# Preparing the S5 tables in batches of eight pairs, and a fourth dense hidden tile, in a hybrid decoder layer

## The chip, the cores and the metric

The kernel runs on one core of one Trainium2 chip. The metric is the device time of one execution in microseconds (us); where several executions were timed, their median. A profiled execution gives a span, from its first to its last recorded instruction, and a time of its own beside it.

## The reference, cut to what matters

The kernel computes one layer for 1024 prompt positions and 8 × 4 sample positions, 1056 columns in all, with 1024 features in fp32.

```python
def swiglu(h, w_gate, w_up, w_down):
    return (jax.nn.silu(h @ w_gate) * (h @ w_up)) @ w_down      # 1024 -> 2816 -> 1024
...
        x = x + 0.5 * swiglu(rmsnorm(x, ffn1_norm[i]), ffn1_w_gate[i], ffn1_w_up[i], ffn1_w_down[i])
        m, s5r, s5i, ssd1, conv1 = mixer(rmsnorm(x, mix_norm[i]), *st, *mix_params)
        x = x + m.astype(x.dtype)
        x = x + 0.5 * swiglu(rmsnorm(x, ffn2_norm[i]), ffn2_w_gate[i], ffn2_w_up[i], ffn2_w_down[i])
...
    y_prompt = rmsnorm(xp, final_norm)
```

The mixer holds a Mamba-2 part and an S5 part, a diagonal complex recurrence of 32 groups × 64 states (16 pairs of groups, two groups side by side on 128 partitions). Before the recurrence runs, tables are made from its parameters alone: powers of e^(i·angle) for 128 steps per pair (`dTab`), input and output factors (`dV`, `dW`) and a short kernel (`dT`).

## The kernel before, in words

Every fp32 product is three passes of TensorE in a rounded fp32 format: each operand is a high part (copied by ScalarE, line L158, function `act`) and a low part (subtracted by VectorE, L145, function `tt`), and the passes are high·high, high·low and low·high. So each weight tile (`wr` raw, `ws` split) and each activation tile costs one ScalarE and one VectorE instruction before TensorE can use it. All DMAs are issued by SyncE in one queue.

Each FFN has 22 hidden tiles of 128. The first `NSTD` = 3 are "old-form" tiles: gate and up weights are multiplied with all eight tiles of x in three blocks of 352 columns (`dense`, lines L307 to L309; the first tile of each FFN by `pair`, L336 to L338), 144 matmuls a tile. The other 19 go through a Strassen-Winograd scheme (`strassen`, L669 to L671): seven products of half size a tile ("unit"), each of 24 matmuls of 264 columns, so 168 a unit. Products run one after the other over all units; each needs combinations of quadrants of x ("11", "1", "21", ...), which the steps of `x_steps` make on VectorE and ScalarE and which live in the same pages (`xn`, `d`, `e`) as everything else. Behind that, `down` multiplies the hidden tiles, read back from DRAM (`dH`) by `h_fetch` and split again, with the down weights in chunks of 8, 8 and 6 hidden tiles; its evacuation (`stt`, L155) adds onto x, which `x_load` has read back.

The order is set by a clock of ticks: after every third matmul the program calls `tick()`, which issues background steps whose gap, in ticks, has run out. Two queues of steps exist; `GAP` holds the gaps by name, and `at(n, fn)` places a step n ticks on. `rs_steps` (the sums for the norm, whose last reduction is the matmul `rs_col`, L369) and `x_steps` run this way under the old-form tiles: `sums(14)` starts them 14 ticks after it is called, behind FFN1's first tile but ahead of FFN2's.

The S5 preparation (`s5_prep`) is one queue of such steps, begun 30 ticks into FFN1's `down`. After the small steps come eight slices of two pairs, each of `vees` (six VectorE operations up to `vr` and `vi`, stored to `dV`, L1191), `kern` (L1200 on TensorE, a ScalarE copy into `kt`, a VectorE addition to it, eight stores to `dT`, L1208), `doubleus` (six more, up to `wr` and `wi`) and `turn` (L1222 transposes, a copy to `we`, a store to `dW`, L1225) and two parts of `table` (L1232 copies, doublings of the table from 1 to 128 steps, one Newton step that restores unit length, a store to `dTab`, L1242). Ahead of `down`'s last chunk, `mid(2)` calls `flush()`: all steps that are still in the queue are issued there, one behind the other, before the next matmul of `down`, and the fetch of the last six hidden tiles behind them.

Of the kernel before, what the change touches and what calls it, by code (L numbers as in the profile page):

```python
# [9 lines left out]
F32 = mybir.dt.float32  # L10
# [12 lines left out]
NH = 22  # L23
# [3 lines left out]
WARM = 9  # L27
HT = T // 2
HB = HT // 2
NSTD = 3  # L30
CHUNKS = (range(0, 8), range(8, 16), range(16, NH))
EPS = 1e-6
RND = 12582912.0
# [3 lines left out]
    rs=14, rs1=1, rs2=1, a=4, b=2, h=4, a3=4, b3=2, h3=8, first=7, second=6, tail0=4, tail1=10, tail2=5, done=6, done2=6, done3=6, done4=6, add=4,  # L37
    a_dec=1, a_exp=2, a_pe=2, a_mul=2, b_pe=2, b_y=1, load_a=3, sample=6, split=18, split2=18, split_hi=5, split_lo=2, v0=1,
    v1=6, v2=6, v3=3, glu1=5, glu2=11, low=5, load=14, t0=12, t1=16, u0=8, u1=12, v_0=7, v_1=14, out=16, zout=2, s5z=6, row=4, s5a=6,
    s5b=5, s5c=6, s5d=4, prep=6, tiny=5,  # L40
)

ORDER = ((0, 1, 5, 2, 3, 6, 4, 7),) * 3 + ((0, 1, 2, 3, 4, 5, 6, 7),)
# [91 lines left out]
class Build:  # L135
# [269 lines left out]

    def std(self, wcol, rsd, first):

        nc = self.nc
        sums = lambda gap: (self.rs_steps(rsd, gap), self.x_steps(wcol))
        Gs = G, U, _ = self.Gs  # L410
        (i, w), (j, v) = self.w_next(), self.w_next()
        if not first:
            sums(14)
        self.pair(self.xn, [(w, lambda b, c0, n, p: self.act(G[:, c0:c0 + n], p, AF.Copy)),
                            (v, lambda b, c0, n, p: nc.vector.tensor_copy(U[:, c0:c0 + n], p))])
        self.w_done(i)
        self.w_done(j)
        if first:
            sums(14)

        def silu():
            self.tt(G, G, self.rs, MUL)
            self.act(G, G, AF.Silu)
            self.tt(U, U, self.rs, MUL, nc.gpsimd)

        def prod():
            self.tt(G, G, U, MUL)
            self.store(self.dH[0], G)

        for h in range(1, NSTD):  # L430
            self.std_tile(h, Gs[(h + 1) % 3], (silu, prod) if h == 1 else ())

    def std_tile(self, h, G, fix):
        nc = self.nc
        i, w = self.w_next()

        def ev_gate(b, c0, n, p):
            c = slice(c0, c0 + n)
            g = self.tmp()  # L440
# [145 lines left out]

    def strassen(self, src, ban=()):
        nc, X, st = self.nc, self.X, {}
        hs = list(range(NSTD, NH))
        n = len(hs)  # L590
        sets = [self.banks[2 * i:2 * i + 2] for i in range(3)]
        last = self.Gs[NSTD % 3]
        one, two = (t for t in self.Gs if t is not last)
        P1s, U2s, VB = one[:, 0:HT], one[:, HT:T], two[:, 0:HT]
        GB, GAs = last[:, HT:T], (two[:, HT:T], last[:, 0:HT])
# [16 lines left out]
        for i in range(1, n):  # L612
            h, p = hs[i], pos["P1", i]
# [35 lines left out]
        for p, (name, i) in enumerate(order):  # L649
            h = hs[i]  # L650
# [4 lines left out]
            a, b, c = st[i]  # L655
# [21 lines left out]
            self.wsp_free.put(w)  # L677
            if i == n - 1:
                self.released(N, src)
        assert not todo, todo.keys()  # L680

    def released(self, N, src):

        for hi, lo in self.X[N]:
            self.pages.put_half(hi, lo)
        if N == "11":
            self.wlim = self.wlims.popleft()
        if N == "21":
# [283 lines left out]
    def weights(self):  # L972
        a = self.a

        def ffn(f):
            gu, dn = a["gu" + f], a["dn" + f]
            s = [(gu[n, j], 1024) for n in range(NSTD) for j in range(2)]
            for ch in CHUNKS:
                for m in range(KD):
                    c = m % 4 * 256  # L980
                    s.append((dn[ch[0] // 2:ch[-1] // 2 + 1, m // 4, :, c:c + 256].rearrange("n p c -> p n c"), 128 * len(ch)))
            return s

        w = a["win"]
        seq = ffn("1")
# [3 lines left out]
        seq += out(1) + out(2) + out(3)  # L989
        n = len(seq)  # L990
        seq += ffn("2")
        self.wlims = deque((2 * NSTD, n + 2 * NSTD, len(seq)))
        return seq

    def s5_prep(self, F):
# [11 lines left out]
        vr, vi = f("vr", 2, 9, 16), f("vi", 2, 9, 16)  # L1008
        t1, t2 = f("t1", 288), f("t2", 288)
        wr, wi = f("wr", 2, 8, 16), f("wi", 2, 8, 16)  # L1010
        we = f("we", 2, 2, 128)
        kt = F.tile([16, 4, 240], F32, name="kt")
# [214 lines left out]
        def table(sl, part):  # L1227
            s2 = slice(2 * sl, 2 * sl + 2)
            c, s = tab[:, :, 0], tab[:, :, 1]
            if part == 0:  # L1230
                for j in range(2):
                    nc.vector.tensor_copy(tab[:, :, j, 0], e8[:, j, s2])  # L1232
            for n in ((1, 2, 4, 8, 16), (32, 64))[part]:
                sh = [128, 2, n]
                u1, u2 = (t[:, 0:2 * n].rearrange("p (g n) -> p g n", n=n) for t in (t1, t2))
                bR, bI = (t[:, :, n - 1:n].broadcast_to(sh) for t in (c, s))
                self.cmul(c[:, :, n:2 * n], s[:, :, n:2 * n], c[:, :, 0:n], s[:, :, 0:n], bR, bI, u1, u2)
                yield 2
            if part == 1:
                u1, u2 = (t[:, 0:256].rearrange("p (g n) -> p g n", g=2) for t in (t1, t2))  # L1240
                self.unit(c, s, u1, u2)
                nc.sync.dma_start(self.dTab[:, s2], tab)  # L1242
# [891 lines left out]
```

## Time and the profile before

| what | value |
|---|---|
| median of three runs | 2414.36 us (2411.01 to 2415.25) |
| profiled execution, own time | 2411.99 us |
| its span | 2410.0 us |
| mean granted clock of TensorE | 0.974 of full speed |
| TensorE busy | 2291.6 us (95%) |
| VectorE busy | 1552.2 us (64%) |
| ScalarE busy | 851.5 us (35%) |
| mean DMA traffic | 114 GB/s |

In the rows PE is TensorE, DVE VectorE, ACT ScalarE, POOL GpSimd, SPq SyncE's DMA issues. The ends of matmuls are modelled, so overlapping matmuls show longer than they are apart: their number in a stretch tells the rate, not their length. A time in brackets behind a row of the timeline is the idle time ahead of it and, behind the arrow, what ended it.

### The profile page before, as it was taken

How to read it: one execution, taken by the hardware profiler on the slowest of the kernel's cores; microseconds unless marked ns; L12 is line 12 of the kernel's file. 1: busy time of each engine (PE TensorE's matmuls, PEld its weight loads, DVE VectorE, ACT ScalarE, POOL GpSimd, SP SyncE). 2: the span in 40 equal slices, each digit the busy share in tenths (PEclk: the TensorE clock that was granted, in tenths of full speed). 3: DMA queues.
4: the chain of work that ended last, by engine and by line, in shares of the span. 5: the costliest groups of instructions: out<-in, count | busy, mean ns of one | idle time of the engine just before them, and what ended most of it. 6: DMA issues, size and time to landing. Idle time of an engine off the chain costs nothing. (4 is left out here: it accounts for less than half of the span.)

```text
span 2410.0 us, 41241 instructions
## 1 busy us (share of the span) xinstructions
PE 2291.6 (95%) x16487; PEld 2225.9 (92%) x16487; DVE 1552.2 (64%) x3298; ACT 851.5 (35%) x1382; POOL 380.4 (16%) x443
## 2 busy tenths in 40 slices
PE   9899999999954999999999999998999999999998
PEld 9799999989944989999999988998999999999997
DVE  6955555567776548688788878876955555552325
ACT  5433333322112213355545555223433333341122
POOL 1000000000000323233242455433100000000003
PEclk9899999999976999999999999999999999999999
DMA  3222122353222145454554654533122222172211
GB/s 134 80 80 80 68 84 71 124 208 98 88 59 96 52 152 164 139 181 145 173 165 146 199 157 132 172 102 124 73 76 80 76 80 73 71 277 65 89 51 72
DMA packets 192125, 274.69 MB, mean 114 GB/s; under 512 B 31551, under 2 KB 137278, under 8 KB 191934
## 3 DMA queue, kind: packets, MB, share of 16 engines
q1 hardware_dynamic: 191358, 271.54, 34.0%
q8 instruction: 129, 2.11, 0.4%
q14 instruction: 62, 0.51, 0.1%
q10 hardware_dynamic: 576, 0.52, 0.1%
HBM read 195.17 MB, written 76.84 MB: 113 GB/s over the span
## 5 line engine op out<-in xcount | busy, mean ns | idle before, releaser
L307 PE MATMUL b<-xn,ws 128*128 128x352 f32 (+3 forms) x1824 | 611.0, 335 | 4.5 <-DVE tb L145 2.5
L308 PE MATMUL b<-xn,ws 128*128 128x352 f32 (+3 forms) x1848 | 598.0, 324 | 2.8 <-DVE xn L155 2.2
L309 PE MATMUL b<-xn,ws 128*128 128x352 f32 (+3 forms) x1824 | 589.6, 323 | 0.0
L307 PEld LDWEIGHTS b<-xn,ws 128*128 128x128 f32 x1824 | 344.6, 189 | 14.9 <-DVE x L145 3.2
L308 PEld LDWEIGHTS b<-xn,ws 128*128 128x128 f32 x1848 | 350.9, 190 | 7.9 <-DVE xn L155 2.8
L670 PE MATMUL b<-xn,ws 128*128 128x264 f32 x1216 | 347.5, 286 | 1.5 <-DVE xn L145 1.5
L671 PE MATMUL b<-xn,ws 128*128 128x264 f32 x1216 | 346.7, 285 | 1.4 <-DVE ws L145 1.4
L669 PE MATMUL b<-xn,ws 128*128 128x264 f32 x1216 | 345.7, 284 | 2.1 <-ACT xn L158 1.0
L309 PEld LDWEIGHTS b<-xn,ws 128*128 128x128 f32 x1824 | 344.7, 189 | 0.0
L145 DVE TENSOR_TENSOR ws<-wr,ws 128x512 fp32r<-128x512 f32 (+3 forms) x208 | 227.0, 1093 | 107.7 <-ACT ws L158 107.7
L145 DVE TENSOR_TENSOR g<-b,g 128x264 f32<-128x264 f32 (+1 forms) x316 | 136.7, 434 | 232.0 <-PE b L671 164.5
L158 ACT ACTIVATE ws<-wr 128x512 fp32r<-128x512 f32 (+3 forms) x208 | 169.5, 818 | 273.6 <-PE b L308 238.1
L669 PEld LDWEIGHTS b<-xn,ws 128*128 128x128 f32 x1216 | 229.3, 189 | 2.7 <-ACT xn L158 1.3
L670 PEld LDWEIGHTS b<-xn,ws 128*128 128x128 f32 x1216 | 228.9, 188 | 2.3 <-DVE xn L145 2.3
L671 PEld LDWEIGHTS b<-xn,ws 128*128 128x128 f32 x1216 | 229.3, 189 | 1.9 <-DVE ws L145 1.9
L669 PE MATMUL b<-d,ws 128*128 128x264 f32 x684 | 195.8, 286 | 2.4 <-ACT ws L158 2.4
L671 PE MATMUL b<-d,ws 128*128 128x264 f32 x684 | 195.7, 286 | 0.7 <-DVE ws L145 0.7
L670 PE MATMUL b<-d,ws 128*128 128x264 f32 x684 | 196.2, 287 | 0.0
L307 PE MATMUL b<-d,ws 128*128 128x352 f32 (+2 forms) x510 | 168.2, 330 | 22.3 <-ACT d L158 16.2
L155 DVE SCALAR_TENSOR_TENSOR x<-b,x 128x352 f32<-128x352 f32 (+2 forms) x144 | 73.5, 522 | 173.0 <-PE b L309 172.7
L309 PE MATMUL b<-d,ws 128*128 128x352 f32 (+2 forms) x510 | 167.5, 328 | 1.3 <-DVE ws L145 1.3
L158 ACT ACTIVATE g<-b 128x264 f32<-128x264 f32 (+1 forms) x234 | 91.5, 391 | 216.2 <-PE b L671 211.8
(416 smaller groups left out, 4350.9 us busy)
## 6 DMA issues: line engine op xcount, KB each, us to landing
wr<-in_gu SPq DMA_DIRECT2D x67, 512.0 KB
dH<-g SPq DMA_DIRECT2D x76, 264.0 KB
wr<-in_win SPq DMA_DIRECT2D x36, 512.0 KB
wr<-in_dn SPq DMA_DIRECT2D x32, 512.0 KB
abc<-dA SPq DMA_DIRECT2D x32, 384.0 KB
xn<-dH SPq DMA_DIRECT2D x21, 528.0 KB
dC<-acc SPq DMA_DIRECT2D x20, 528.0 KB
xb<-dC SPq DMA_DIRECT2D x32, 320.0 KB
```

What stands on the lines that cost most here:

```text
L145: (eng or self.nc.vector).tensor_tensor(out, x, y, op=op)
L155: self.nc.vector.scalar_tensor_tensor(out, x, s, y, op0=op0, op1=op1)
L158: self.nc.scalar.activation(out, x, f, **k)
L307: nc.tensor.matmul(p, wh[:, kc], xh, start=(k == 0), stop=False)
L308: nc.tensor.matmul(p, wh[:, kc], xl, start=False, stop=False)
L309: nc.tensor.matmul(p, wl[:, kc], xh, start=False, stop=(k == K - 1))
L669: nc.tensor.matmul(q, wh, xh, start=(k == 0 and name in ("P1", "P2", "P5")), stop=False, skip_group_check=True)
L670: nc.tensor.matmul(q, wh, xl, start=False, stop=False, skip_group_check=True)
L671: nc.tensor.matmul(q, wl, xh, start=False, stop=(k == 3), skip_group_check=True)
```

## The change

FFN1 gets a fourth old-form tile and 18 Strassen units; FFN2 keeps three, but its sums start 40 ticks on and not 14. In the last unit of the last product, the pump of weights (`w_pump`) is called after each product that ends a unit, so that down weights are loaded and split there. The eight reloads of x now start after 24 ticks and are 18 ticks apart; before, they started at once, 6 apart. In `s5_prep` the tables are made first, eight pairs at a time in two halves, and the slices hold only `vees`, `doubleus`, `kern`, `turn`, with gaps of 4 for 6; the small steps have gaps of 3 for 5. The tiles of the slices and those of the tables share one tile, `pad`: the table (`tab`) its columns 0 to 2047, temporaries 2048 to 3071, and the slices' `vr`, `vi`, `t1`, `t2`, `wr`, `wi`, `we` columns 0 to 2175, `kt` 2176 to 3135.

```diff
-NSTD = 3
+NSTD = 4, 3
...
-    s5b=5, s5c=6, s5d=4, prep=6, tiny=5,
+    s5b=5, s5c=6, s5d=4, prep=4, tiny=3, table=2,
...
         if not first:
-            sums(14)
+            sums(40)
...
             self.wsp_free.put(w)
             if i == n - 1:
                 self.released(N, src)
+                if len(self.units[h]["done"]) == 7:
+                    self.w_pump()
...
         if N == "21":
             for m in range(KD):
-                self.at(6 * m, lambda m=m: self.x_load(m, src))
+                self.at(24 + 18 * m, lambda m=m: self.x_load(m, src))
...
+        pad = f("pad", 3136)
+        place = lambda c0, *s: pad[:, c0:c0 + int(np.prod(s))].rearrange("p (a b c) -> p a b c", b=s[1], c=s[2])
...
+        def table(half):
+            s8 = slice(8 * half, 8 * half + 8)
             c, s = tab[:, :, 0], tab[:, :, 1]
+            for j in range(2):
+                nc.vector.tensor_copy(tab[:, :, j, 0], e8[:, j, s8])
+            for n in (1, 2, 4, 8, 16, 32, 64):
+                sh = [128, 8, n]
...
+                yield GAP["table"] * (1 + n // 16)
+            for i in range(2):
+                u1, u2 = (t.rearrange("p (g n) -> p g n", g=4) for t in tmp)
+                self.unit(c[:, 4 * i:4 * i + 4], s[:, 4 * i:4 * i + 4], u1, u2)
+                yield 4 * GAP["table"]
+            nc.sync.dma_start(self.dTab[:, s8], tab)
...
+        for half in range(2):
+            L(GAP["tiny"], lambda half=half: table(half))
+        L(GAP["tiny"], lambda: nc.gpsimd.memset(kt, 0.0))
         for sl in range(8):
-            for fn in (vees, kern, doubleus, turn):
+            for fn in (vees, doubleus, kern, turn):
                 L(GAP["prep"], lambda fn=fn, sl=sl: fn(sl))
-            for part in range(2):
-                L(GAP["prep"], lambda sl=sl, part=part: table(sl, part))
```

VectorE at the end of `down`'s second chunk, before: `x7` with banks `b3` to `b5` is the chunk's last evacuation, and what follows it is a table.

```order
L145 TENSOR_TENSOR t2_4924<-tab_4931 128x32
L145 TENSOR_TENSOR tab_4931<-t1_4923,t2_4924 128x2x16
L155 SCALAR_TENSOR_TENSOR x7_96<-b3_68,x7_96 128x352
L155 SCALAR_TENSOR_TENSOR x7_96<-b4_69,x7_96 128x352
L155 SCALAR_TENSOR_TENSOR x7_96<-b5_70,x7_96 128x352
L145 TENSOR_TENSOR t1_4923<-tab_4931 128x64
L145 TENSOR_TENSOR t2_4924<-tab_4931 128x64
L145 TENSOR_TENSOR tab_4931<-t2_4924,t1_4923 128x2x32
```

VectorE at the same place after: the low parts of the last chunk's hidden tiles (`d5`, `d0`, ...) follow the evacuations directly.

```order
L155 SCALAR_TENSOR_TENSOR x7_96<-b3_68,x7_96 128x352
L155 SCALAR_TENSOR_TENSOR x7_96<-b4_69,x7_96 128x352
L155 SCALAR_TENSOR_TENSOR x7_96<-b5_70,x7_96 128x352
L145 TENSOR_TENSOR d5_163<-d5_163,d2_160 128x1056
L145 TENSOR_TENSOR d0_158<-d0_158,d8_166 128x1056
L145 TENSOR_TENSOR ws4_105<-wr1_100,ws3_104 128x768
L145 TENSOR_TENSOR d6_164<-d6_164,d3_161 128x1056
```

What moved: between the last evacuation of the second chunk and the first low part of the third, no preparation step is left.

VectorE in the new kernel where the second half of the tables ends and the first slice begins (`pad` is both; `128x512` are the Newton step of four pairs, `128x288` is `vees`).

```order
L145 TENSOR_TENSOR pad_4872<-pad_4872 128x512 x3
L152 TENSOR_SCALAR pad_4872<-pad_4872 128x512
L145 TENSOR_TENSOR pad_4872<-pad_4872 128x4x128 x2
L145 TENSOR_TENSOR d0_158<-d0_158,xn15_88 128x1056
L145 TENSOR_TENSOR d6_164<-d6_164,d3_161 128x1056
L155 SCALAR_TENSOR_TENSOR x7_96<-b3_68,x7_96 128x352
L155 SCALAR_TENSOR_TENSOR x7_96<-b4_69,x7_96 128x352
L145 TENSOR_TENSOR pad_4872<-s5par_4844,pwi_4869 128x288
L145 TENSOR_TENSOR pad_4872<-s5par_4844,pwr_4868 128x288
L145 TENSOR_TENSOR pad_4872<-pad_4872 128x288
L155 SCALAR_TENSOR_TENSOR x7_96<-b5_70,x7_96 128x352
```

And TensorE in the new kernel at the first slice's `kern` (L1206 there): it stands in the middle of `down`'s matmuls.

```order
L308 MATMUL b2_67<-xn12_85,ws2_103 128x352
L309 MATMUL b2_67<-xn11_84,ws5_106 128x352
L1206 MATMUL b6_71<-pad_4872,bbr_4866 16x128 x4
L1206 MATMUL b6_71<-pad_4872,bbi_4867 16x128 x4
L307 MATMUL b0_65<-xn13_86,ws2_103 128x352
L308 MATMUL b0_65<-xn14_87,ws2_103 128x352
```

What moved: all matmuls of `down` behind this place now stand behind the whole of both table halves on VectorE, and behind the end of the second half's store, since `vees` writes columns of `pad` that the store reads.

SyncE at the end of FFN1's Strassen part, before: reloads of x stand between the fetches of hidden tiles (`d5`, `xn4`, ...).

```order
L709 DMA xn3_76<-dH0_127 128x1056
L698 DMA x2_91<-in_x 128x1056
L709 DMA d5_163<-dH0_127 128x1056
L698 DMA x3_92<-in_x 128x1056
L246 DMA wr0_99<-in_dn1 128x4x256
L698 DMA x4_93<-in_x 128x1056
L709 DMA xn4_77<-dH0_127 128x1056
```

SyncE at the same place after:

```order
L712 DMA xn3_76<-dH0_127 128x1056
L712 DMA d5_163<-dH0_127 128x1056
L246 DMA wr0_99<-in_dn1 128x4x256
L701 DMA x0_89<-in_x 128x1056
L712 DMA xn4_77<-dH0_127 128x1056
L712 DMA xn6_79<-dH0_127 128x1056
L712 DMA xn8_81<-dH0_127 128x1056
```

What moved: one reload of x stands where five stood, the others come later in `down`, and the hidden tiles follow each other.

Counted in ticks from the start of FFN1: before, `down` begins at tick 1208, the preparation at 1238, and the last chunk at 1592, with three slices' rest still in the queue. After, `down` begins at 1200, the preparation at 1230, the two table halves stand at 1293 to 1337 and 1340 to 1384, the first slice's `vees` at 1391, its `kern` at 1401, a slice every 18 ticks from there, the last step at 1531 and the last chunk at 1584.

## Rows read from the trace of the kernel before

**Rows 1.** The page: span, TensorE's busy time.

```profile
span 2410.0 us, 41241 instructions
...
PE 2291.6 (95%) x16487; PEld 2225.9 (92%) x16487; DVE 1552.2 (64%) x3298; ACT 851.5 (35%) x1382; POOL 380.4 (16%) x443
```

**Rows 2.** Windows by stage: engines' busy us (instructions), granted clock, DMA share.

```profile
core 0: us, PE busy (x) PEld busy (x) DVE busy (x) ACT busy (x) POOL busy (x), PEclk, DMA share, GB/s
...
80.00:120.00 40.00, 28.95 (x176) 26.80 (x175) 36.61 (x59) 21.37 (x42) 1.27 (x1) 0.79 0.20 67
120.00:480.00 360.00, 360.00 (x2954) 360.00 (x2953) 188.88 (x350) 127.25 (x263) 0.00 (x0) 1.00 0.23 83
...
489.00:510.00 21.00, 15.81 (x79) 15.02 (x78) 8.82 (x9) 8.77 (x10) 0.89 (x1) 0.84 0.92 352
510.00:691.00 181.00, 179.64 (x1176) 176.31 (x1175) 135.16 (x512) 28.51 (x45) 3.55 (x16) 1.00 0.28 85
691.00:759.00 68.00, 9.40 (x67) 3.95 (x66) 51.01 (x214) 7.61 (x18) 0.00 (x0) 0.53 0.26 78
759.00:766.00 7.00, 6.60 (x29) 6.61 (x30) 6.98 (x7) 4.68 (x5) 0.00 (x0) 0.67 0.66 254
766.00:830.00 64.00, 64.00 (x399) 64.00 (x398) 36.95 (x36) 20.67 (x21) 15.74 (x6) 1.00 0.12 38
1663.00:1700.00 37.00, 32.58 (x188) 31.90 (x187) 23.52 (x33) 13.03 (x18) 7.67 (x3) 0.91 0.13 45
1742.00:1772.00 30.00, 30.00 (x247) 30.00 (x246) 21.89 (x40) 13.46 (x28) 0.00 (x0) 1.00 0.23 84
...
2134.00:2160.00 26.00, 23.12 (x134) 22.62 (x134) 15.01 (x16) 10.41 (x11) 0.00 (x0) 0.93 0.68 259
```

**Rows 3.** Timeline of TensorE around the flush: start, us, instruction, [idle before].

```profile
691.62 0.32 PE L309 MATMUL b<-d,ws 128*128 128x352 f32 x1
699.28 0.62 PE L1200 MATMUL b<-vr,bbr 64*16 64x128 f32 x8 [7.33 <-DVE vr L145]
...
717.05 0.62 PE L1200 MATMUL b<-vr,bbr 64*16 64x128 f32 x8 [11.07 <-DVE vr L145]
...
758.10 0.66 PE L307 MATMUL b<-d,ws 128*128 128x352 f32 x1 [16.19 <-ACT d L158]
```

**Rows 4.** Timeline of VectorE in the flush: one slice's rest and its table.

```profile
702.42 0.21 DVE L145 TENSOR_TENSOR kt<-kt,kd 16x64 f32<-16x64 f32 x1 [1.81 <-ACT kt L158]
...
704.93 0.23 DVE L1232 COPY tab<-e 128x2 f32<-128x2 f32 x2
705.20 0.23 DVE L145 TENSOR_TENSOR t<-tab 128x2 f32<-128x2 f32 x2
...
705.66 0.23 DVE L145 TENSOR_TENSOR t<-tab 128x2 f32<-128x2 f32 x2
...
713.15 0.76 DVE L145 TENSOR_TENSOR t<-tab 128x256 f32<-128x256 f32 x2
...
715.52 0.46 DVE L145 TENSOR_TENSOR t<-s5par,pwi 128x288 f32<-128x288 f32 x1
```

**Rows 5.** Timelines of SyncE and ScalarE behind the flush.

```profile
751.89 1.83 SPq L709 DMA_DIRECT2D d<-dH  x4
...
756.97 1.08 ACT L158 ACTIVATE d<-d 128x1056 fp32r<-128x1056 f32 x1 [13.63 <-DMA d<-dH]
```

**Rows 6.** VectorE's groups by shape, 490 to 760 us: busy us, mean ns.

```profile
L155 DVE SCALAR_TENSOR_TENSOR x<-b,x 128x352 f32<-128x352 f32 x48 | 24.6, 522 | 30.9 <-PE b L309 30.8
L145 DVE TENSOR_TENSOR ws<-wr,ws 128x1024 fp32r<-128x1024 f32 x16 | 19.4, 1220 | 11.9 <-ACT ws L158 11.9
...
L145 DVE TENSOR_TENSOR xn<-xn,xn 128x1056 fp32r<-128x1056 f32 x5 | 6.0, 1252 | 0.0
```

**Rows 7.** Timeline of TensorE at three other waits.

```profile
92.21 0.59 PE L670 MATMUL b<-e,ws 128*128 128x264 f32 x1 [3.27 <-DVE e L145]
...
493.47 0.43 PE L307 MATMUL b<-d,ws 128*128 128x352 f32 x1 [3.93 <-ACT ws L158]
...
1674.34 3.17 PE L369 MATMUL b<-ones,acc 128*128 128x1 f32 x18 [4.29 <-POOL acc L145]
```

More of the change, by code (lines that the diff above doesn't have):

```diff
@@ L406, in std @@
     def std(self, wcol, rsd, first):
-        nc = self.nc
+        nc, n = self.nc, NSTD[not first]
+        self.nstd = n
         sums = lambda gap: (self.rs_steps(rsd, gap), self.x_steps(wcol))
@@ L428, in prod @@
             self.store(self.dH[0], G)
-        for h in range(1, NSTD):
+        for h in range(1, n):
             self.std_tile(h, Gs[(h + 1) % 3], (silu, prod) if h == 1 else ())
@@ L449, in std_tile @@
         i, w = self.w_next()
-        last = h == NSTD - 1
+        last = h == self.nstd - 1
         if last:
@@ L453, in std_tile @@
             self.rs_free()
-            self.later(2, lambda: self.unit_load(NSTD), 1)
-            for fn in self.unit_first(NSTD):
+            self.later(2, lambda: self.unit_load(self.nstd), 1)
+            for fn in self.unit_first(self.nstd):
                 self.later(2, fn, 1)
-            self.at(10, lambda: self.unit_load(NSTD + 1))
+            self.at(10, lambda: self.unit_load(self.nstd + 1))
         def ev_up(b, c0, n, p):
@@ L588, in strassen @@
         nc, X, st = self.nc, self.X, {}
-        hs = list(range(NSTD, NH))
+        hs = list(range(self.nstd, NH))
         n = len(hs)
         sets = [self.banks[2 * i:2 * i + 2] for i in range(3)]
-        last = self.Gs[NSTD % 3]
+        last = self.Gs[self.nstd % 3]
         one, two = (t for t in self.Gs if t is not last)
@@ L976, in ffn @@
             gu, dn = a["gu" + f], a["dn" + f]
-            s = [(gu[n, j], 1024) for n in range(NSTD) for j in range(2)]
+            s = [(gu[n, j], 1024) for n in range(NSTD[int(f) - 1]) for j in range(2)]
             for ch in CHUNKS:
@@ L991, in weights @@
         seq += ffn("2")
-        self.wlims = deque((2 * NSTD, n + 2 * NSTD, len(seq)))
+        self.wlims = deque((2 * NSTD[0], n + 2 * NSTD[1], len(seq)))
         return seq
@@ L1007, in s5_prep @@
         rvr, rvi = f("rvr", NPAIR, 8), f("rvi", NPAIR, 8)
[L1008 to L1012, printed above, removed]
+        pad = f("pad", 3136)
+        place = lambda c0, *s: pad[:, c0:c0 + int(np.prod(s))].rearrange("p (a b c) -> p a b c", b=s[1], c=s[2])
+        vr, vi = place(0, 2, 9, 16), place(288, 2, 9, 16)
+        t1, t2 = pad[:, 576:864], pad[:, 864:1152]
+        wr, wi = place(1152, 2, 8, 16), place(1408, 2, 8, 16)
+        we = place(1664, 2, 2, 128)
+        kt = pad[0:16, 2176:3136].rearrange("p (a b) -> p a b", b=240)
+        tab = place(0, 8, 2, 128)
+        tmp = pad[:, 2048:2560], pad[:, 2560:3072]
         kd = F.tile([16, 4, 16], F32, name="kd")
         e8 = f("e8", 2, NPAIR)
-        tab = f("tab", 2, 2, 128)
         self.dV = D.tile([128, NPAIR, 2, 128], F32, name="dV")
@@ L1051, in load @@
             nc.sync.dma_start(dsk, a["s5d"])
-            nc.gpsimd.memset(kt, 0.0)
         def mag():
@@ L1225, in turn @@
             nc.sync.dma_start(self.dW[:, 2 * sl:2 * sl + 2], we)
-        def table(sl, part):
-            s2 = slice(2 * sl, 2 * sl + 2)
+        def table(half):
+            s8 = slice(8 * half, 8 * half + 8)
             c, s = tab[:, :, 0], tab[:, :, 1]
[L1230 to L1235, printed above, removed]
+            for j in range(2):
+                nc.vector.tensor_copy(tab[:, :, j, 0], e8[:, j, s8])
+            for n in (1, 2, 4, 8, 16, 32, 64):
+                sh = [128, 8, n]
+                u1, u2 = (t[:, 0:8 * n].rearrange("p (g n) -> p g n", n=n) for t in tmp)
                 bR, bI = (t[:, :, n - 1:n].broadcast_to(sh) for t in (c, s))
                 self.cmul(c[:, :, n:2 * n], s[:, :, n:2 * n], c[:, :, 0:n], s[:, :, 0:n], bR, bI, u1, u2)
[L1238 to L1242, printed above, removed]
+                yield GAP["table"] * (1 + n // 16)
[4 more added lines that the diff above has]
+            nc.sync.dma_start(self.dTab[:, s8], tab)
         L(6, load)
```

## The prediction

> **What bounds the kernel now.** First the page: TensorE is busy for 2291.6 of a span of 2410.0 us [rows 1], so the chain that ends last is nearly all matmuls, and a change can gain only what TensorE loses in some stage, or save matmuls. It saves none to speak of. Second, windows by stage, read by the number of matmuls in each: at full rate 2954 of 264 columns take 360 us, 0.1219 us apart, and 399 of 352 columns take 64 us, 0.1604 apart [rows 2]. A stretch's loss is its length less its number times that distance. Third, the timeline of TensorE where a window falls short, to see what ended each wait. The stages that the change touches lose this much.
>
> - The start of FFN1's Strassen part, 80 to 120 us: 40 − 176 × 0.1219 = 18.5 us, at a granted clock of 0.79 while VectorE is busy 36.6 of 40 [rows 2]. Single waits are for VectorE's low parts (3.27 us for `e` [rows 7]). FFN2's start, 1742 to 1772, runs at 247 in 30 us and loses nothing [rows 2].
> - The start of `down`: 21 − 79 × 0.1604 = 8.3 us in FFN1 and 26 − 134 × 0.1604 = 4.5 in FFN2 [rows 2]. It begins with a wait of 3.93 us for a down weight's high part [rows 7], while FFN1's DMA engines are 0.92 busy and move 352 GB/s; in part the clock is low (0.84 and 0.93) [rows 2].
> - The flush: nothing of `down` runs from 691.94 (691.62 and the row's 0.32) to 758.10 [rows 3], which is 66.2 us, and the restart costs 758.10 to 766 less 30 matmuls or so, about 2.9 at a clock of 0.67 [rows 2]: 69.1. In it VectorE works without a break, and a slice comes every 717.05 − 699.28 = 17.8 us [rows 3], of which its table takes 704.93 to 715.52, 10.6 us, and the rest 7.2, 1.8 of that a wait for ScalarE's `kt` [rows 4]. Behind the last step the fetch of hidden tiles is issued at 751.89, ScalarE gets the first one at 756.97 [rows 5], and VectorE's low part follows.
> - FFN2's first tiles, 1663 to 1700: 188 instructions, 18 of them the one-column `rs_col`, which take 3.2 us; 37 − 3.2 − 170 × 0.1604 = 6.5 us are lost, 4.29 of them in front of `rs_col`, for an addition of POOL [rows 2, 7], the rest at a low clock behind it.
>
> **The change, part by part.** All sums are against the profiled execution, 2411.99 us (1.99 above its span); the median of the three runs, 2414.36, is 2.4 above that. A measurement of this kernel tells about 0.2% (5 us) from no change.
>
> *A, the preparation.* By the order the last step now stands 53 ticks ahead of the last chunk, so nothing is left to flush, and 69.1 us fall away. Against this stand four costs.
> First, three slices' transposes and small matmuls move under `down`, but still cost TensorE time. Five slices cost the stretch 510 to 691 in all 181 − 1076 × 0.1604 = 8.4 us (1176 less some 100 small ones [rows 2]), at most 1.7 each; I take 1.0 each, 3.0.
> Second, the last chunk still has to wait for its first hidden tile's low part, which now stands right behind the chunk's last evacuation on VectorE. Its transfer (5.1 us from issue to ScalarE's copy [rows 5]) is covered by the last 24 ticks, 11.5 us, of the chunk; the split's 1.25 us [rows 6] and the evacuations ahead of it are not: 2.0.
> Third, the new wait. TensorE takes its instructions in order, and the first slice's `kern` needs `vees`, which stands on VectorE behind both table halves. A table instruction costs a fixed part and a part by columns: three of 2 columns take 705.66 − 705.20 = 0.46 us, and the last six of the table, 256 wide, 715.52 − 713.15 = 2.37 [rows 4], so 0.155 + 0.00094 a column. Checked on the old table, 50 instructions with 3060 columns: 7.75 + 2.9 = 10.6, as measured. A new half has 56 instructions (2 copies, 7 doublings of 6, 2 Newton steps of 6) with 6 × 8 × 127 + 12 × 512 = 12240 columns: 8.7 + 11.5 = 20.2 us. So VectorE's tables fall from 8 × 10.6 = 85 to 40.4, but they come in one stretch. Between the tables' start at tick 1293 and the `kern` at 1401 lie 108 ticks of three matmuls, 108 × 0.481 = 52.0 us. VectorE has to do in it 40.4 of tables, 2.6 of `vees`, 13 evacuations × 0.522, 4 weights × 1.22 and 3 hidden tiles × 1.25 [rows 6], in sum 58.5. Besides it waits twice for a store of 1.05 MB out of `pad`, once before the second half's first copy and once before `vees`. No row shows such a store; from below it is nothing (VectorE is late anyway, and has other work first), from above the 5.1 us of the fetch, twice its size perhaps 7 [rows 5]. Nearer is the fetch, being a DMA of the same queue: 5 the first time, when three ticks lie between, and 2 the second. 58.5 + 7 − 52.0 = 13.5 us of waiting (bounds 6.5 and 24, the upper with the powers' burst of some 3 us ahead).
> Fourth, behind a wait of this length the clock falls, as behind the flush: the ramp lost 7 − 29 × 0.1604 = 2.3 us [rows 2]; I take 2.5.
> The slices themselves should fit. One has 18 ticks, 8.7 us, and 1.0 of its own on TensorE, and asks of VectorE 5.4 (7.2 − 1.8), 2.25 evacuations and three quarters of a weight and of a hidden tile, 1.2 and 1.9: 8.5. The wait for `kt` lies behind `doubleus` now. A = 69.1 − 3.0 − 2.0 − 13.5 − 2.5 = 48.1 us.
>
> *B, the fourth tile.* It costs 144 × 0.1604 = 23.1 us for a unit's 168 × 0.1219 = 20.5, so 2.6 more. It gives VectorE 23 us under which x is still being combined, of which its own evacuations and weights take about 6; so the backlog of the start, where waits and a low clock cost 18.5, shrinks by 17. I leave 1.0: B = 18.5 − 1.0 − 2.6 = 14.9 (6 left would give 10).
>
> *C, `down`'s start.* With three weights split up to 16 ticks earlier the first matmul's wait of 3.93 goes, and with seven of the eight reloads of x (1056 columns, 0.54 MB each) out of the way the DMA engines deliver hidden tiles sooner. x is first needed at the first evacuation, 24 ticks into `down`, and is in by then since each reload comes 18 ticks behind the last and each evacuation 24: no new wait. I leave 1.5 in each FFN: 8.3 − 1.5 + 4.5 − 1.5 = 9.8 (from below 4, if the transfers were the bound and only the weight's wait in FFN1 goes).
>
> *D, FFN2's sums.* 26 ticks later is 12.5 us, against POOL's lateness of 4.29 [rows 7]: the wait and the slow matmuls behind it go, 6.5 − 0.5 = 6.0. The steps that combine x start as much later, under two more tiles; if that made FFN2's Strassen start late, D would be 0 or below.
>
> Sum: 48.1 + 14.9 + 9.8 + 6.0 = 78.8; 2412.0 − 78.8 = 2333.2, and a median lies nearer the runs' middle: **2334**.
>
> [...]
>
> **The rivals.**
> *The backlog is absorbed.* If the stores cost VectorE nothing and the first wait doesn't lower the clock, A gains 7 + 2.5 more, and with C and B without remainder another 5: 2319. For it: VectorE idles 27 of 64 us in the third chunk [rows 2], so it has slack outside of the burst. Against: the sum of 58.5 over 52.0 holds without any store.
> *VectorE stays the bound in the slices.* If the wait for `kt` isn't hidden, a slice asks 8.5 + 1.8 = 10.3 of 9.7, and if each store costs 7, the first `kern` waits 10 longer: 8 × 0.6 + 10 = 15 less: 2349. For it: VectorE was 135 of 181 busy in 510 to 691 already [rows 2], with five slices in it and not eight.
> *The boundaries gain nothing.* The old waits of C are replaced by waits for hidden tiles, whose transfers are the same, and D moves the lateness to FFN2's Strassen start: 78.8 − 9.8 − 6.0 = 63 gained: 2350.
> *Slower than before: the slices serialise.* All slices use one `kt`, one `vr` and one `wr`, so each waits for the stores and steps of the one before. In the flush a slice's rest takes 7.2 us when all engines serve it alone [rows 3, 4]; if between `down`'s evacuations each of eight took a wait of TensorE of 10 us (79 / 8), all would be lost, and the clock, 0.53 in the flush [rows 2], would stay low and cost up to 8 × 9 more. It decides at 10 us a slice: 2414, and 2450 at 15. Against: the five slices before cost 1.7 each at most, with longer gaps.
>
> **How the numbers follow.** My forecast, its sum within some 9 us, 0.52; absorbed 0.14; VectorE bound 0.17; boundaries nothing 0.11; serialised 0.04, and 0.02 for a smaller loss elsewhere that leaves no change. The likeliest case's own range is 2324 to 2344. For 8 in 10 I reach from 2314 (absorbed, with the stretches of bounds) to 2358 (VectorE bound or boundaries nothing, 8 above). Faster 0.94, same 0.02, slower 0.04.
>
> **What would show it.** Right: no long break of TensorE ahead of the last chunk; in `down`'s first chunks eight `kern` groups some 10 us apart; one wait of about 13 us for `vr`'s successor in `pad` ahead of the first, with VectorE continuously busy for 50 us and idle rows of about 5 and 2 us behind the two stores; Strassen starting at full rate; the wait of `rs_col` for POOL gone. Wrong: waits of several us ahead of each `kern` or transpose; waits for hidden tiles or x at the start of `down`; a late x in FFN2's first products; a hole of any length where the flush was.

## The result and the profile after

The changed kernel takes 2346.36 us (median of 4 runs, 2343.33 to 2346.87) where the one before takes 2413.9: a ratio of 0.9719, 95% interval 0.9702 to 0.9736, so 67.5 us less. The forecast was 2334, in a range of 2314 to 2358, with 78.8 us gained; the time lies inside that range, but 2 us above what the prediction called the likeliest case's own range (2324 to 2344), and nearer to two of its rivals (2349 and 2350) than to 2334. So the time alone does not tell which of them came true; the rows by stage do. The profiled execution took 2343.33 with a span of 2341.6; the spans differ by 68.4.

The page of the changed kernel first, as [rows 1]:

```profile
span 2341.6 us, 40890 instructions
...
PE 2281.7 (97%) x16463; PEld 2221.4 (95%) x16463; DVE 1508.9 (64%) x2998; ACT 846.1 (36%) x1372; POOL 385.2 (16%) x446
```

Then the windows of the changed kernel by stage, the columns as in [rows 2]. Here too 2298 matmuls of 264 columns in 280 us and 369 of 352 columns in 59 us give the full rates, 0.1218 and 0.1599.

```profile
105.00:125.00 20.00, 16.63 (x120) 16.42 (x119) 18.30 (x33) 10.38 (x22) 0.00 (x0) 0.88 0.30 107
160.00:440.00 280.00, 280.00 (x2298) 280.00 (x2297) 146.36 (x271) 99.40 (x209) 0.00 (x0) 1.00 0.23 79
470.00:484.00 14.00, 12.05 (x94) 11.41 (x93) 10.34 (x14) 8.77 (x12) 0.00 (x0) 1.00 0.82 306
484.00:500.00 16.00, 13.22 (x81) 12.69 (x80) 8.36 (x9) 8.14 (x9) 0.00 (x0) 1.00 0.89 324
...
584.00:600.00 16.00, 3.67 (x26) 2.52 (x25) 15.01 (x26) 1.08 (x4) 0.89 (x1) 0.62 0.33 115
600.00:697.00 97.00, 97.00 (x688) 93.76 (x687) 56.63 (x133) 21.89 (x46) 0.00 (x0) 0.99 0.41 116
697.00:710.00 13.00, 11.34 (x67) 10.53 (x66) 10.22 (x12) 5.86 (x7) 0.00 (x0) 1.00 0.47 168
710.00:769.00 59.00, 59.00 (x369) 59.00 (x368) 36.11 (x34) 19.48 (x21) 15.72 (x6) 1.00 0.15 45
1600.00:1626.00 26.00, 25.86 (x167) 25.47 (x166) 12.65 (x20) 9.43 (x13) 7.76 (x3) 1.00 0.13 50
1672.00:1690.00 18.00, 12.34 (x77) 11.62 (x77) 17.79 (x32) 11.71 (x24) 0.00 (x0) 0.81 0.31 100
...
2071.00:2095.00 24.00, 24.00 (x153) 24.00 (x152) 15.60 (x20) 9.07 (x10) 0.00 (x0) 1.00 0.72 254
```

Read by number times distance, with the distances of [rows 2] so that both sides are measured alike, the stages lose:

| stage | before | after | gain | forecast |
|---|---|---|---|---|
| A: S5 preparation under `down`, and the last chunk's start | 8.4 + 69.1 = 77.5 | 14.4 + 9.7 + 2.3 = 26.4 | 51 | 48.1 |
| B: FFN1's Strassen start, less the tile's 2.6 | 18.5 | 5.4 | 10.5 | 14.9 |
| C: start of `down`, FFN1 and FFN2 | 8.3 + 4.5 | 3.0 + 0 | 9.8 | 9.8 |
| D: FFN2's first tiles (`rs_col` in it) and its Strassen start | 9.7 + 0 | 2.1 + 8.6 | −1.0 | 6.0 |

(A after: of the 26 matmuls in 584 to 600, 16 are `kern`'s, so 16 − 10 × 0.1604; of the 688 behind, 144 are small, so 97 − 544 × 0.1604; and 13 − 67 × 0.1604. In D, `rs_col` is left in on both sides: 37 − 170 × 0.1604 and 26 − 149 × 0.1604.) The table sums to 70; two smaller losses that it leaves out, 1.5 in FFN1's old-form tiles and 2 at the end of its Strassen part, bring it to 67, near the 68.4. Where the prediction was out, it was in B and D, and both times at the start of a Strassen part.

The wait that the prediction had put ahead of the first `kern` is there. On TensorE in the changed kernel (`issue` in a bracket means that the profile names nothing that ended the wait):

```profile
584.03 0.32 PE L309 MATMUL b<-xn,ws 128*128 128x352 f32 x1
594.64 0.63 PE L1206 MATMUL b<-pad,bbr 64*16 64x128 f32 x8 [10.28 <-issue]
597.31 0.63 PE L1206 MATMUL b<-pad,bbi 64*16 64x128 f32 x8 [2.05 <-DVE pad L155]
```

And on VectorE, without the rows between, the second table half and its two neighbours:

```profile
559.66 1.29 DVE L145 TENSOR_TENSOR pad<-pad 128x512 f32<-128x512 f32 x2
560.88 0.51 DVE L155 SCALAR_TENSOR_TENSOR x<-b,x 128x352 f32<-128x352 f32 x1
564.97 0.25 DVE L1237 COPY pad<-e 128x8 f32<-128x8 f32 x2 [3.58 <-DMA dTab<-pad]
...
587.86 1.29 DVE L145 TENSOR_TENSOR pad<-pad 128x512 f32<-128x512 f32 x2
589.07 1.25 DVE L145 TENSOR_TENSOR d<-d,xn 128x1056 fp32r<-128x1056 f32 x1
590.24 1.25 DVE L145 TENSOR_TENSOR d<-d,d 128x1056 fp32r<-128x1056 f32 x1
...
593.11 0.46 DVE L145 TENSOR_TENSOR pad<-s5par,pwi 128x288 f32<-128x288 f32 x1 [0.75 <-DMA dTab<-pad]
...
593.97 0.46 DVE L145 TENSOR_TENSOR pad<-pad 128x288 f32<-128x288 f32 x1
...
596.80 0.46 DVE L155 SCALAR_TENSOR_TENSOR pad<-pad 128x288 f32<-128x288 f32 x1
```

VectorE is late all the way: the second half ends only at 589.07, almost five us after TensorE stopped, two hidden tiles' low parts stand between it and `vees`, and only then does `kern` run. That `kern` waits for `vees` is read from the times: the last operation on `vr` ends at 594.43 (593.97 and 0.46), 0.2 us ahead of `kern`'s start. VectorE waits for both stores, 3.58 and 0.75 us, where the forecast had 5 and 2. The seven `kern` groups behind the first come 9.9 us apart or so, as forecast. At the last chunk's start nothing of the 66-us hole is left; a wait of 1.6 us for one low part is.

### The profile page after: what moved, and what is told of

The parts are those of the page before. It is cut to its first block, busy times and chain, and to the rows that moved or that the text cites. A ratio compares the mean times of both kernels' runs of the same rounds, so it can differ in the third digit from the quotient of the medians.

```text
span 2341.6 us, 40890 instructions
## 1 busy us (share of the span) xinstructions
PE 2281.7 (97%) x16463; PEld 2221.4 (95%) x16463; DVE 1508.9 (64%) x2998; ACT 846.1 (36%) x1372; POOL 385.2 (16%) x446
## 5 line engine op out<-in xcount | busy, mean ns | idle before, releaser
L307 PE MATMUL b<-xn,ws 128*128 128x352 f32 (+3 forms) x1872 | 628.3, 336 | 6.0 <-DVE tb L145 2.3
L308 PE MATMUL b<-xn,ws 128*128 128x352 f32 (+4 forms) x1896 | 614.4, 324 | 3.3 <-DVE xn L155 2.2
L309 PE MATMUL b<-xn,ws 128*128 128x352 f32 (+3 forms) x1872 | 606.0, 324 | 0.0
L672 PE MATMUL b<-xn,ws 128*128 128x264 f32 x1184 | 339.4, 287 | 1.9 <-DVE ws L145 1.9
L670 PE MATMUL b<-xn,ws 128*128 128x264 f32 x1184 | 336.6, 284 | 4.0 <-ACT g L158 4.0
L671 PE MATMUL b<-xn,ws 128*128 128x264 f32 x1184 | 338.4, 286 | 0.0
L145 DVE TENSOR_TENSOR ws<-wr,ws 128x512 fp32r<-128x512 f32 (+4 forms) x206 | 225.0, 1093 | 97.0 <-ACT ws L158 97.0
L158 ACT ACTIVATE ws<-wr 128x512 fp32r<-128x512 f32 (+4 forms) x206 | 169.2, 823 | 276.8 <-PE b L308 222.6
L672 PE MATMUL b<-d,ws 128*128 128x264 f32 x666 | 190.9, 287 | 4.9 <-DVE ws L145 4.9
L670 PE MATMUL b<-d,ws 128*128 128x264 f32 x666 | 190.0, 285 | 0.8 <-ACT ws L158 0.8
L671 PE MATMUL b<-d,ws 128*128 128x264 f32 x666 | 190.0, 285 | 0.0
L307 PE MATMUL b<-d,ws 128*128 128x352 f32 (+2 forms) x510 | 165.5, 325 | 0.0
L309 PE MATMUL b<-d,ws 128*128 128x352 f32 (+2 forms) x510 | 164.5, 323 | 0.0
```

The source lines that it names most:

```text
L145: (eng or self.nc.vector).tensor_tensor(out, x, y, op=op)
L158: self.nc.scalar.activation(out, x, f, **k)
L307: nc.tensor.matmul(p, wh[:, kc], xh, start=(k == 0), stop=False)
L308: nc.tensor.matmul(p, wh[:, kc], xl, start=False, stop=False)
L309: nc.tensor.matmul(p, wl[:, kc], xh, start=False, stop=(k == K - 1))
L670: nc.tensor.matmul(q, wh, xh, start=(k == 0 and name in ("P1", "P2", "P5")), stop=False, skip_group_check=True)
```

## The experiments

Each was timed with the kernel before on the same chip. Times are medians.

**The S5 preparation alone.** The kernel before, with the new `s5_prep` and its gaps:

```diff
-    s5b=5, s5c=6, s5d=4, prep=6, tiny=5,
+    s5b=5, s5c=6, s5d=4, prep=4, tiny=3, table=2,
... (and s5_prep as in the change)
```

> The kernel before with the new S5 preparation alone. If the terms of the parts simply add (the flush's 69 us go, some 18 to 20 come back as three slices' small matmuls, one wait of about 11 us ahead of the first kern and its ramp): 2414 - 50 = 2364. If the preparation's part needs the other edits (x reloads and late weights fall into the same stretch and make VectorE later there): 2370 to 2380.

2364.55 against 2414.33 (ratio 0.9793, 0.9777 to 0.9810): 49.8 us, term A as forecast within 2, and some three quarters of the whole gain. Its trace has the same two waits ahead of and in the first `kern`, 10.27 and 2.05 us. The part needs no help from the others.

**Closer steps without batches.** Two numbers in the kernel before:

```diff
-    s5b=5, s5c=6, s5d=4, prep=6, tiny=5,
+    s5b=5, s5c=6, s5d=4, prep=3, tiny=3,
```

> The kernel before with two gaps smaller (prep 3 for 6, tiny 3 for 5): tables still by two pairs inside each slice, eight slices 34 ticks apart, the last step 22 ticks ahead of the last chunk, so nothing is flushed. If VectorE's work decides, each slice asks it for 10.6 of table, 5.4 of its own and about 5.7 of down's work in 17.4 us (34 ticks and TensorE's own 1.0), 21.7 in all: waits of about 4 us a slice, 35 in all, some of them at a low clock, and 2414 - 69 + 35 + 8 = 2388 (2378 to 2398). If only the number of ticks decided, nothing would be left of the flush and no burst would come first: 2350 to 2355, faster than or like the changed kernel's S5 part alone.

2392.88 (ratio 0.9915, 0.9900 to 0.9929). The hole at the last chunk is gone here as well, but TensorE now waits in every slice. On TensorE in this kernel, two of the slices, and a window with seven of the eight:

```profile
550.99 0.62 PE L1200 MATMUL b<-vr,bbr 64*16 64x128 f32 x8 [3.84 <-issue]
...
574.57 0.62 PE L1200 MATMUL b<-vr,bbr 64*16 64x128 f32 x8 [2.55 <-DVE vr L145]
576.14 0.62 PE L1200 MATMUL b<-vi,bbi 64*16 64x128 f32 x8 [0.95 <-DVE vi L155]
```

```profile
510.00:700.00 190.00, 164.92 (x1011) 156.59 (x1012) 155.22 (x607) 30.75 (x54) 3.70 (x16) 0.90 0.29 86
```

So emptying the queue in time is worth 21 us, and the new `s5_prep` 28 more (2392.9 − 2364.6). The batches of eight pairs are what lowers VectorE's work there: by the pages of the two runs it is busy for 1513.0 us with the new `s5_prep` and for 1548.2 with this one. But the new one also makes the tables ahead of the slices, puts `doubleus` ahead of `kern` and has other gaps, and no run has the batches alone. What this run shows by itself is that the number of ticks is not enough: with the queue empty in time, TensorE waits for VectorE's `vr` and `vi` in each slice.

**The first slice later.**

```diff
-        L(GAP["tiny"], lambda: nc.gpsimd.memset(kt, 0.0))
+        L(GAP["tiny"] + 28, lambda: nc.gpsimd.memset(kt, 0.0))
```

> The changed kernel with the first slice 28 ticks later (13.5 us), so that VectorE can finish the tables and the second store before kern; the last step then stands 25 ticks ahead of the last chunk. If the wait of 10.4 us ahead of the first kern, the 2.3 behind it and the low clock around it are VectorE's lateness from the two table halves alone: they go, 2346 - 13 = 2333 (2331 to 2337). If VectorE is the bound of the whole stretch, the lateness only moves to later slices or to the chunk's end: 2344 to 2348.

2337.77 (ratio 0.9684, 0.9670 to 0.9698), 8.6 below the changed kernel and not 13. The wait ahead of `kern` is gone, but VectorE's lateness shows in the next thing that TensorE needs from it, a hidden tile's low part:

```profile
593.50 0.66 PE L308 MATMUL b<-d,ws 128*128 128x352 f32 x1 [4.31 <-DVE d L145]
```

On VectorE in this kernel that low part stands behind the same Newton steps:

```profile
590.98 1.29 DVE L145 TENSOR_TENSOR pad<-pad 128x512 f32<-128x512 f32 x2
592.19 1.25 DVE L145 TENSOR_TENSOR d<-d,xn 128x1056 fp32r<-128x1056 f32 x1
```

Neither theory had it right: of some 13 us, 8.6 went with `kern`'s wait and the slow clock behind it, and 4.3 came back where the next instruction needed VectorE, which is still late from the tables there.

**The tables spread out.**

```diff
-    s5b=5, s5c=6, s5d=4, prep=4, tiny=3, table=2,
+    s5b=5, s5c=6, s5d=4, prep=4, tiny=3, table=3,
```

> The changed kernel with the table's gap 3 for 2: each half takes 66 ticks (31.8 us) for 44, VectorE's 20.2 of table and some 11 of down's own fit in them, and the last step stands 9 ticks ahead of the last chunk. If the wait ahead of the first kern, and the 4.3 us for a hidden tile's low part that stayed when only the slices were put later, are both the burst on VectorE: 2346 - 15 = 2331, 6 below the later slices' 2337.8. If VectorE has not that slack: like the later slices, 2337 or above.

2338.19 (ratio 0.9682, 0.9668 to 0.9696): the burst's waits are gone, as the first theory has it, but the time is that of the later slices. A new wait took the rest. The last slice now ends 9 ticks ahead of the last chunk, and on SyncE its stores stand ahead of the fetch of the last hidden tiles; TensorE's first matmul of the chunk waits for them. SyncE, then TensorE, in this kernel:

```profile
680.45 4.64 SPq L1214 DMA_DIRECT2D dT<-pad  x8
685.14 0.43 SPq L246 DMA_DIRECT2D wr<-in_dn  x1
685.67 0.44 SPq L1231 DMA_DIRECT2D dW<-pad  x1
686.20 1.92 SPq L712 DMA_DIRECT2D d<-dH  x4
```

```profile
692.15 0.66 PE L307 MATMUL b<-d,ws 128*128 128x352 f32 x1 [6.24 <-ACT d L158]
```

In the changed kernel that fetch is issued from 687.40 on, 9 us ahead of the chunk's start at 696.9. That the queue's order is the cause is read from these rows; no run moved the stores alone.

**Three old-form tiles in FFN1 again.**

```diff
-NSTD = 4, 3
+NSTD = 3, 3
```

> The changed kernel with three old-form tiles in FFN1 again. By the prediction's term B the fourth tile is worth 14.9: 2346 + 15 = 2361. By the two traces (18.8 us lost at the Strassen part's start before; 6.7 after, 1.5 more in the old-form tiles and 2.6 for the tile itself) it is worth 8: 2354.

2352.94 (ratio 0.9749, 0.9735 to 0.9764): the fourth tile is worth 6.6 us, not 14.9. The loss at the Strassen start is there again (the waits are for `e`, `xn` and a weight, as in the kernel before, 3.3 us the longest), with a clock of 0.72:

```profile
83.00:113.00 30.00, 18.94 (x94) 16.79 (x94) 26.79 (x42) 14.67 (x29) 1.40 (x1) 0.72 0.22 71
```

**Five old-form tiles in FFN1.**

```diff
-NSTD = 4, 3
+NSTD = 5, 3
```

> The changed kernel with a fifth old-form tile in FFN1. The fourth one measured 6.6 us and left 6.7 at the Strassen part's start. If what is left is still backlog of VectorE, one more tile takes it away for 2.6: 2346 - 6 + 3 = 2343. If it is a wait within the Strassen part's own first products (ScalarE behind VectorE at the first silu), it stays and the tile's 2.6 are added: 2349.

2336.42 (ratio 0.9684, 0.9671 to 0.9697), 10 below the changed kernel: more than the 3 that the first theory gave, and clear against the second. The Strassen part starts at full rate:

```profile
127.00:147.00 20.00, 20.00 (x166) 20.00 (x165) 15.96 (x29) 11.34 (x24) 0.00 (x0) 1.00 0.22 81
```

By the phases of the two traces FFN1 up to `down` is 6.7 shorter and what lies between there and FFN2 1.9; the other 1.4 lie within what medians of four runs differ by.

**A fourth tile in FFN2.**

```diff
-NSTD = 4, 3
+NSTD = 4, 4
```

> The changed kernel with a fourth old-form tile in FFN2 as well (sums still 40 ticks on). If FFN2's Strassen start (9 us lost) waits for VectorE's backlog of combining x, 23 more us of tiles absorb it, for 2.6: 2346 - 9 + 3 = 2340. If the backlog only moves with the tile, as it partly did in FFN1 (6.7 left there): 2346 to 2348.

2339.81 (ratio 0.9687, 0.9670 to 0.9704), 6.5 below: the 8.6 us lost at FFN2's Strassen start are gone for the tile's 2.6. That start in this kernel:

```profile
1701.00:1721.00 20.00, 20.00 (x165) 20.00 (x164) 15.96 (x29) 11.34 (x24) 0.00 (x0) 1.00 0.23 80
```

The five times reach from 2331.64 to 2343.50, and the profiled execution is the longest of them, as long as the changed kernel's 2343.33. FFN2 up to the end of its Strassen part takes 464.9 us in its trace for 470.9 in the changed kernel's, 6.0 less; FFN1 and what lies between, which the edit leaves as they are, took that much longer in this execution. So the 6 us rest on FFN2's rows more than on the medians.

**FFN2's sums where they were, and halfway.**

```diff
-            sums(40)
+            sums(14)
```

> The changed kernel with FFN2's sums 14 ticks on again, as before. By the prediction's term D the later sums are worth 6.0: 2352. By the two traces the later sums give back what they gain (7.6 us less lost in FFN2's first tiles, but 6.9 more lost at the start of its Strassen part, where VectorE is behind): 2346 to 2348.

2341.43 (ratio 0.9707, 0.9693 to 0.9721). With the sums at 14 the wait for POOL is back, and FFN2's Strassen part starts at full rate, both as before:

```profile
1609.70 3.44 PE L369 MATMUL b<-ones,acc 128*128 128x1 f32 x18 [4.28 <-POOL acc L145]
```

```profile
1678.00:1698.00 20.00, 20.00 (x166) 20.00 (x165) 15.96 (x29) 11.34 (x24) 0.00 (x0) 1.00 0.22 82
```

From FFN2's first matmul to the last of its Strassen part the changed kernel's trace takes 1600.2 to 2071.1, 470.9 us, and this one's 1598.1 to 2068.0, 469.9; the kernel before takes 471.7. So the later sums gain nothing; that they cost 5, as the medians have it, the stage itself doesn't show, and the intervals overlap.

```diff
-            sums(40)
+            sums(27)
```

> The changed kernel with FFN2's sums 27 ticks on, halfway. POOL was 4.3 us late at 14 ticks; 13 ticks are 6.3 us. If the loss in the first tiles is POOL's lateness alone it goes here too, and if FFN2's Strassen start suffers from each tick by which the combining of x is put off, half of its 6.9 us come back: 2342 to 2344. If the Strassen start's loss is there at any delay, or the wait for POOL comes back: 2346 to 2349.

2346.24 (ratio 0.9725, 0.9711 to 0.9738): no halfway gain. The first tile is 6.1 us shorter than with the sums at 14 (27.1 for 33.2 by the phases of the two traces), but a wait of 1.8 us for ScalarE stands behind it and the Strassen part is 6 longer; FFN2 up to the end of that part takes 473.3 for 469.9. So the loss at the Strassen start is there at 27 ticks as at 40, as the second theory has it; where between 14 and 27 it begins, no run shows.

**C, each half undone.** First the reloads of x at once again, then no early weights:

```diff
-                self.at(24 + 18 * m, lambda m=m: self.x_load(m, src))
+                self.at(6 * m, lambda m=m: self.x_load(m, src))
```

> The changed kernel with the eight reloads of x at once and 6 ticks apart again, in both FFNs; the down weights stay early. The two traces give 9.8 us for both edits at the start of down (9.8 and 7.7 lost before, 6.2 and 1.5 after). If the transfers in the way of the hidden tiles are half of it: 2346 + 4 = 2350 or more. If the weight's wait was all of it: 2346.

2348.35 (ratio 0.9725, 0.9712 to 0.9738), 2.0 slower than the changed kernel, too little to be told from it by medians. The rows are clearer. With the reloads in the way, the wait for a hidden tile's high part in FFN1 is 4.94; in the changed kernel the same wait is 1.75 (first row this kernel, then, in the second fence, the changed one):

```profile
497.77 0.66 PE L307 MATMUL b<-xn,ws 128*128 128x352 f32 x1 [4.94 <-ACT xn L158]
```

```profile
495.61 0.43 PE L307 MATMUL b<-xn,ws 128*128 128x352 f32 x1 [1.75 <-ACT xn L158]
```

```diff
-                if len(self.units[h]["done"]) == 7:
-                    self.w_pump()
```

> The changed kernel without the pump of weights in the last unit; reloads of x stay 18 ticks apart. Before, the first matmuls of down waited 3.9 and 0.7 us for a weight's high and low part in FFN1 and 2.2 and 0.7 in FFN2. If the early weights are what took these away, they come back with their low clock: 2346 + 6 = 2352. If the free DMA queue alone brings the weights in time: 2346.

2349.62 (ratio 0.9731, 0.9718 to 0.9744), 3.3 slower. The waits for the weight's two parts come back, in FFN1 shorter than in [rows 7], in FFN2 as they were (2.21 there in the kernel before too):

```profile
486.00 0.61 PE L307 MATMUL b<-d,ws 128*128 128x352 f32 x1 [2.37 <-ACT ws L158]
...
2074.37 0.43 PE L307 MATMUL b<-d,ws 128*128 128x352 f32 x1 [2.21 <-ACT ws L158]
```

**The gains together.**

```diff
-NSTD = 4, 3
+NSTD = 5, 4
...
-    s5b=5, s5c=6, s5d=4, prep=4, tiny=3, table=2,
+    s5b=5, s5c=6, s5d=4, prep=4, tiny=3, table=3,
```

> Five old-form tiles in FFN1, four in FFN2, the table's gap 3. If the three gains add (10 for the fifth tile, 6.5 for FFN2's fourth, 15 for the wider gap): 2346 - 31 = 2315. If they take from the same lateness or meet a new limit: 2320 to 2328.

2324.45 (ratio 0.9622, 0.9608 to 0.9635): 22 us below the changed kernel and 90 below the one before. With the wider gap's measured 8 in place of 15 the three would add to 24.7, so they nearly do (the medians of single kernels are told apart to some 4 us). Its largest wait under `down` is again the last chunk's, 5.19 us for a hidden tile.

## Why the prediction was right, and where it was short

*A held, step by step.* Forecast 48.1, measured 49.8 alone. The waits ahead of and in the first `kern` were given 13.5 and are 10.28 + 2.05 = 12.3; the stores' share in it, 7 in the forecast, is 4.3 (3.58 and 0.75), so that the rest is 8.0 and not 6.5. No run has the tables and the slices in tiles of their own, so what the stores cost is read from these two rows alone. The slow clock behind the wait, 2.5 in the forecast, costs about 2.0, at a granted clock of 0.56: between 597.87 and 601.85 TensorE starts 12 matmuls of 352 columns and four small ones, and 12 × 0.1604 is 1.9. The last chunk's start loses 2.3 for 2.0. The price of a table half, 0.155 us an instruction and 0.00094 a column from rows of 2 to 256 columns, gave 20.2; the second half takes 564.97 to 589.07, 24.1, less 4.0 of other rows in between: 20.1. The slices fit between `down`'s evacuations: (9.7 + the first one's share) / 8, some 1.3 us each with the slow clock behind the first, where the forecast had 8.4 + 3.0 for eight, 1.4 each. The rival of VectorE as the bound of the slices and the slower one of slices in series are both out, the latter by a factor of 8. That VectorE is what decides was tested with its work raised again: with tables by pairs under close steps TensorE waits for it in each slice, and the kernel is 28 us slower than with the new `s5_prep`.

*C held nearly in its sum.* 9.8 was forecast and the windows at the start of `down` give 9.8; in FFN2 nothing is left, in FFN1 3.0 and not 1.5. But the late part of FFN1's Strassen work, 470 to 484, loses 14 − 94 × 0.1219 = 2.5 us in small waits, where 470 to 489 lost 0.6 before (151 matmuls in 19 us), so some 2 of the 9.8 are given back; that the weights and fetches moved there cause them is likely and was not tested. Undone one at a time the two edits cost 2.0 and 3.3, neither clear of what medians differ by; no run undid both. By the medians the other three parts together give 18.2 us beyond the preparation alone (2364.55 − 2346.36); less the fourth tile's 6.6 that leaves 11.6 for C and D.

*B failed in its size.* The step "the backlog of the start shrinks by 17; I leave 1.0" left too little. The waits for `e`, `xn` and a weight are gone, as it expected; but one wait of another kind stays, with a fall of the clock behind it (0.51 from 120 to 125). On TensorE in the changed kernel:

```profile
120.82 0.59 PE L670 MATMUL b<-xn,ws 128*128 128x264 f32 x1 [3.37 <-ACT g L158]
```

ScalarE's row shows why its `g` came so late:

```profile
118.27 0.64 ACT L158 ACTIVATE g<-g 128x528 f32<-128x528 f32 x1 [7.17 <-DVE g L145]
```

ScalarE stood 7.17 us before a silu whose input VectorE had still to make, and the evacuations behind it stood too. VectorE's work on x can begin only when the norm's sums are back from DRAM, at 51.30, and from 62 to the start of the Strassen part, at 105.6, it is busy for 42.61 of 43 us: the fourth tile's time is used up, and VectorE is still late. The step had set VectorE's backlog equal to the 18.5 us that TensorE lost by it; but TensorE made 176 matmuls in that stretch, so the backlog could be longer than the loss. VectorE in the changed kernel where it first uses the norm's sums and where it first prepares a Strassen weight (`acc`), then the window between:

```profile
51.30 0.95 DVE L145 TENSOR_TENSOR tb<-b,rs 128x352 f32<-128x352 f32 x2 [5.08 <-DMA rs<-rsd]
...
99.29 0.68 DVE L145 TENSOR_TENSOR acc<-wr 128x512 f32<-128x512 f32 x1
```

```profile
62.00:105.00 43.00, 43.00 (x269) 43.00 (x269) 42.61 (x56) 16.17 (x28) 9.03 (x6) 1.00 0.25 87
```

With the fifth tile it has time to spare, and waits for TensorE just ahead of the same step:

```profile
115.49 0.53 DVE L145 TENSOR_TENSOR tb<-b,rs 128x352 f32<-128x352 f32 x1 [3.33 <-PE b L309]
115.93 0.68 DVE L145 TENSOR_TENSOR acc<-wr 128x512 f32<-128x512 f32 x1
```

There the step stands 11.0 us ahead of the first Strassen matmul, at 126.92, and in the changed kernel 6.3 ahead of 105.59. So what was left was VectorE's lateness, and the fifth tile, with which it goes, shows it. The tile's worth of 6.6 by the clock is less than the 10.5 of the windows. Of the 3.9 between them 0.7 lie in the 20 us behind 125 (158 matmuls), and 1.5 in the second old-form tile, which takes 26.9 us here and 25.3 in the kernel before; but the trace with FFN2's sums at 14, whose FFN1 is the same program, has 25.3 as well, so that this part differs from one execution to the next and is not the tile's. The rest lies within what medians differ by.

*D failed.* The term counted the 6.5 us that the later sums save and left what they delay as a condition ("if that made FFN2's Strassen start late, D would be 0 or below"). It was the case: 26 ticks later means that x is combined 12.5 us later, and VectorE, 17.79 of 18 us busy there, delivers a weight's low part 4.12 us late with a clock of 0.81:

```profile
1681.82 0.59 PE L672 MATMUL b<-d,ws 128*128 128x264 f32 x1 [4.12 <-DVE ws L145]
```

The step that failed is the size of 6.0, which took it that a start that lost nothing before had 12.5 us in hand. That was never shown; the row of 247 matmuls in 30 us [rows 2] tells that there was no loss, not how far off one was. The rival "the boundaries gain nothing" was right for D and wrong for C.

*What the price of a table instruction is made of.* The 0.155 us an instruction fit these tables (20.1 for a half against 20.2), but they are a mean over two kinds of instruction. Three of 2 columns take 0.46 us [rows 4]. Two of them do not depend on each other (705.20, two in 0.23 us, each 0.16 long), and the second starts 0.07 behind the first. The third reads what both wrote, and starts 0.04 behind their end; the next one, at 705.66, overwrites what the third reads, and starts 0.03 behind its end:

```profile
705.47 0.16 DVE L145 TENSOR_TENSOR tab<-t,t 128x2 f32<-128x2 f32 x1
```

At 256 columns it is the same: two in 0.76 us (713.15), each 0.42 long, start 0.34 apart. So two instructions in three wait here for the end of the one before and one in three does not; 0.155 is the price of this mixture, and work with another share of dependent instructions was not priced.

## What to carry to other kernels

A stage that loses nothing says nothing of its slack: before putting its inputs off, find when they were ready, and count the delay against that. Background work needs two budgets, the issue slots (ticks) and the time of the engine that does it; here slots alone gave 21 of 50 us, and the rewrite that lowered the engine's time the rest. A stage's lost time is not the backlog of the engine that it waited for: the loss was 18.5 us, and 23 us more under old-form tiles took away only part of it. When a wait is removed by moving work later, look along each queue at the new place, DMA issues too: with the tables spread out the last chunk's fetch stood behind stores that no engine of the main path needed, and TensorE waited 6.24 us for it.

## What was not expected of the hardware

```profile
560.99 0.33 SPq L1248 DMA_DIRECT2D dTab<-pad  x1
...
589.18 0.32 SPq L1248 DMA_DIRECT2D dTab<-pad  x1
```

A store of 1.05 MB to DRAM released its source 4.0 us after its issue (560.99 to 564.97), and the second one 3.9 (589.18 to 593.11), sooner than the 5.1 us from issue to use of a fetch of 0.54 MB in [rows 5], from which I had taken 5 to 7; that fetch was one of four issued together, so the two are not quite alike. And VectorE's price for an instruction on a table of eight pairs, with strides of 256 elements between the pairs, was in the mean that of the two-pair table (20.1 us for a half, 20.2 by that price): nothing was paid for eight short runs in place of two.
